# Keeping two more head operands in DRAM between their making and their use

## The chip, the cores and the metric

The kernel runs on one core of a Trainium2 chip. The metric is the device time of one execution in microseconds. Before the change the median of three runs is 1178.21 us (1176.94 to 1178.62). A core has TensorE (PE) for matmuls, VectorE (DVE), ScalarE (ACT), GpSimd (POOL) and SyncE (SP); in this kernel SP issues the loads from DRAM and POOL the stores to it.

## The reference

One layer of a hybrid decoder trunk: 1024 tokens, 1024 channels, float32. The input is normalised and modulated, then one large projection makes the operands of two mixers that run side by side: HGRN2 with 8 heads and GLA (gated linear attention) with 4. Each GLA head has a query, a key (128 channels each), a value (256 channels), an output gate, and a decay alpha for every token and key channel:

```python
log_a = jax.nn.log_sigmoid((ga @ alpha_w + alpha_b)) / GLA_GATE_TAU
# per head: S_t = diag(exp(log_a_t)) S_{t-1} + k_t v_t^T,  o_t = S_t^T (scale * q_t)
o = chunked_gated_linear_attention(q, k, v, log_a, GLA_HEAD_K ** -0.5)
o = rms_norm(o, norm_w)
return o.reshape(B, T, GLA_VAL) * jax.nn.silu(gz)
```

Both mixers' outputs are projected, merged by sigmoid gates, projected once more, added to the input and normalised. Heads are counted from 0 here: the third GLA head is head 2, the fourth head 3.

## The kernel before

**Stages.** Features lie on the partitions, 1024 tokens along a row, so an operand of one head (query, key, decay) is one tile of 128 x 1024 float32, 512 KB. After the normalisation the kernel makes the queries of all heads and the first two keys, and stores them in DRAM (qk_d). Then one stream of jobs runs, `stream.go()`: 14 half products of a first value stage, four jobs for output gates of heads 0 and 1, two jobs for the keys of heads 2 and 3 (`gla_k`), 14 half products of a second value stage, 14 of a third stage, and more gate jobs. Afterwards come the merge stages (L1422) and the output stage (L1599).

Each stage of 14 half products forms one large matrix product from seven smaller ones, numbered 1, 2, 5, 3, 6, 7, 4 in this order (L32), each in two halves (`Vjob`, L1912). A half product is 24 matmuls of 128 x 512 at L2000. A float32 operand is split for PE in two parts: a cast on ACT makes the high part (L211) and a subtraction on DVE the low part (L212). Products 1, 2 and 3 of a half have to split only the weights, two parts; the others also the activations, four parts.

**Side work.** Between the jobs' pieces, `weave` (L881) advances generators: the heads one after another (`gla_attention`, L998, then the HGRN2 heads), sums of weights for the later value stages (`v_sums`, L1819: loads at L1829, sums from L1831, stores at L1839), the decays of heads 2 and 3 (`alpha_side`, L934), and sums for the merge stages (`prepare`, L1280). It counts units, one for each piece of a job, four to a half product. A head begins with copies and products of query and decay (L657 to L661), then 64 small score matmuls (L665) that read the key; it ends with an inverse root of the squares of its outputs (`inverse_root`, L985: split at L202 and L203, matmuls L992 and L993, ACT at L994 and L995). A head, when its values are done with, issues the loads of the next head's operands (`load_qk`, L1050, DMA at L1054).

**The slots.** All large tiles live in 46 slots of 4 KB a partition (`Slots`, L37). `get` takes the slot that has been free for longest, `free` returns one; a tile that is being stored counts as freed four units later in that order, though it can be taken at once. A transfer or an instruction that writes a slot waits for the last reader or store of what lay there.

**Look-ahead.** `Stream.ahead` (L853) loads and splits jobs before their turn. For a job that isn't the running one, a load is issued only if the free slots reach the tiles it loads plus four, a split only if they reach its parts plus one:

```python
if d > loads or d > 0 and room() < job.raws + 4:
    break
...
if d > preps or d > 0 and room() < job.parts + 1:
    break
```

`v_sums` waits for eight free slots, `alpha_side` for six, `prepare` for eleven; `prepare` stands still through the second and most of the third stage.

**Order.** After the first part of the program, instructions are put on their engines' queues by the framework's own scheduling, from program order, priorities (evictions of the value stages are preferred) and what it holds ready, except where the kernel pins them. Each engine then takes its queue in order, SP and POOL too.

**Keys and decays.** Queries of all heads and keys of heads 0 and 1 lie in DRAM until `load_qk`. Key 3 does too (k3_d). Key 2 stays in its slot from the end of its job until head 2 ends; the decays of heads 2 and 3 stay in theirs from `alpha_side` on.

Of the kernel before, what the change touches and what calls it, by code (L numbers as in the profile page):

```python
# [10 lines left out]
F32 = mybir.dt.float32  # L11
# [5 lines left out]
P = 128  # L17
D = 1024
T = 1024
# [70 lines left out]
def hybrid_trunk_kernel(  # L90
# [6 lines left out]
    nc = tc.nc  # L97
# [5 lines left out]
    dp = ctx.enter_context(tc.tile_pool(name="dram", bufs=1, space=bass.MemoryType.DRAM))  # L103
# [3 lines left out]
    S = Slots(sp, N_SLOTS)  # L107
# [7 lines left out]
    def mtile():  # L115
        cnt[0] += 1
        return ps_m.tile([P, 512], F32, tag="m", name=f"pm{cnt[0]}")
# [197 lines left out]
    NG = 6  # L315
# [39 lines left out]
    g_state = {}  # L355
# [31 lines left out]
    def mm_alpha(pz, h, sl):  # L387
        for n in range(2):
            nc.tensor.matmul(pz, aw4[:, n, h * P:h * P + P], ga4[:, sl], start=(n == 0), stop=(n == 1))
# [116 lines left out]
    qk_d = [dp.tile([P, T], F32, name=f"qk{f}") for f in range(NG)]  # L506
# [395 lines left out]
    alphas = {}  # L902
# [6 lines left out]
    def alpha_half(half):  # L909
# [21 lines left out]
            nc.scalar.activation(alphas[h][:, sl], m[:, h, :], AF.Exp, scale=1.0 / TAU)  # L931
        S.free(z, m)

    def alpha_side(pair):  # L934
        zs = {}
        while len(S.free_list) < 6:
            yield 1
        for h in pair:
            zb = zs[h] = S.get([T])
            for th in range(2):  # L940
                pz = mtile()
                mm_alpha(pz, h, slice(th * 512, th * 512 + 512))
                nc.scalar.activation(zb[:, th * 512:(th + 1) * 512], pz, AF.Identity,
                                     bias=vec[:, R_AB + h:R_AB + h + 1])
            yield 2
        S.free(ga4, aw4)
        for h in pair:
            m = alphas[h] = S.get([T])
            nc.vector.tensor_scalar_min(m, zs[h], 0.0)
            nc.vector.scalar_tensor_tensor(zs[h], m, 2.0, zs[h], ALU.mult, ALU.subtract)  # L950
            yield 2
        for h in pair:
            nc.scalar.activation(zs[h], zs[h], AF.Exp)
        yield 3
        for h in pair:
            nc.scalar.activation(zs[h], zs[h], AF.Ln, bias=one_t)
            nc.vector.tensor_sub(alphas[h], alphas[h], zs[h])
            yield 2
        for h in pair:
            nc.scalar.activation(alphas[h], alphas[h], AF.Exp, scale=1.0 / TAU)  # L960
            S.free(zs[h])
        yield 3

    def silu_done(store, key):
# [33 lines left out]
    def gla_attention(h):  # L998
# [29 lines left out]
        if h < 3:  # L1028
            load_qk(h + 1)
# [15 lines left out]
                settle(qk, ("z", h, vh))  # L1045
        S.free(*sq.values())

    k3_d = dp.tile([P, T], F32, name="k3")

    def load_qk(h):  # L1050
        for f, key in ((h, "q"), (4 + h, "k")):
            if f < NG or h == 3:
                t = g_state[key, h] = S.get([T])
                nc.sync.dma_start(t, qk_d[f] if f < NG else k3_d)  # L1054

    def gla_k_done(h):
        def f(ps):
            t = S.get([T])
            for th in range(2):
                nc.vector.tensor_copy(t[:, th * 512:th * 512 + 512], ps[th])  # L1060
            if h == 3:
                nc.gpsimd.dma_start(k3_d, t)
                S.free(t, sent=True)
            else:
                g_state[("k", h)] = t
        return f

    def col(c0, w=P):
# [946 lines left out]
    def first_head():  # L2015
        for h in range(4):
            start_side(gla_attention(h))

    vjobs[0][10].begins = lambda: load_qk(0)
    vjobs[0][12].begins = first_head  # L2020

# [23 lines left out]
    def front():  # L2045
        alpha = [alpha_half(half) for half in range(2)]
        for i, _ in enumerate(first_group()):
            if i < 10 and i % 2 == 0:
                next(alpha[0], None)
            if i == 15:  # L2050
                for _ in make_ga(1):
                    pass
                load_wq(0, 0)
                load_wq(1, 0)
            elif i in (16, 17, 18, 20, 22):
                next(alpha[1], None)
            elif i == 19:
                stream.ahead(0, 0, 0)
        for n, z in enumerate(("12", "22")):
            xq[z] = [hT[1, 2 * n + kk] for kk in range(2)]  # L2060
        stream.more.append([v_sums(1), 1, 1, 56])
        stream.more.append([v_sums(2), 1, 1, 56])
        stream.more.append([gate_side(), 4, 1, 300])
        stream.back.append([alpha_side((2, 3)), 1, 1, 86])
        stream.back.append([prepare(), 1, 1, 98])
# [39 lines left out]
```

## Time and profile before

| | |
|---|---|
| median of 3 runs | 1178.21 us |
| the profiled execution | 1176.48 us |
| its span in the trace | 1174.8 us |
| granted PE clock, mean | 0.998 |
| DMA, mean | 209 GB/s, 245.56 MB |
| DVE subtractions at L212 | 92, 1221 ns each |
| ACT casts at L211 | 92, 1048 ns each |

How to read it: the page gives each engine's busy time and share of the span; the windows give the same for chosen stretches; the waits say which engine stood idle until what; the timeline lists instructions in order, with the idle time of the engine before each in square brackets and what ended it. A row with a count such as x2 is several instructions merged. A landing time is from a DMA's issue to its completion.

### The profile page before, as it was taken

The page shows a single profiled execution, that of the slowest core. Times are in us where ns is not written, and L with a number is a line of the kernel's source. Part 1 is how long each engine was busy: PE and PEld are TensorE (multiplying, and loading weights), DVE is VectorE, ACT ScalarE, POOL GpSimd, SP SyncE. Part 2 cuts the span into 40 slices and gives each one's busy share as a digit, 9 for nine tenths or more (in the row PEclk, how much of TensorE's full clock was granted, in tenths as well). Part 3 has the DMA queues.
Part 4 walks back from the last instruction along what each step waited for, and adds up shares of the span by engine and source line. Part 5 has one row for each costly group of instructions (what it writes and reads, how often), then busy time and mean ns, then how long its engine had stood idle before and what let it go on. Part 6 is the DMA issues. An engine that isn't in the chain of part 4 may idle for free.

```text
span 1174.8 us, 20553 instructions
## 1 busy us (share of the span) xinstructions
PE 1148.9 (98%) x8089; PEld 942.3 (80%) x8089; DVE 842.1 (72%) x1316; ACT 646.8 (55%) x963; POOL 138.3 (12%) x285
## 2 busy tenths in 40 slices
PE   7999999999899999999999999999999999999997
PEld 5777888888778888788788888888888888888886
DVE  4755677676686737897697896595543866988994
ACT  5675454284574758646455445566643644534654
POOL 5121111010111101222211110001110000000000
PEclk9999999999999999999999999999999999999999
DMA  9847459486676446988766955156699846435523
GB/s 320 284 151 245 144 193 310 147 281 218 215 247 210 174 142 215 292 279 271 259 205 197 302 164 162 55 172 202 233 321 296 273 155 220 126 109 174 170 95 136
DMA packets 155986, 245.56 MB, mean 209 GB/s; under 512 B 10139, under 2 KB 107473, under 8 KB 155890
## 3 DMA queue, kind: packets, MB, share of 16 engines
q1 hardware_dynamic: 134866, 174.10, 47.3%
q0 software_dynamic: 20976, 70.15, 15.6%
q8 instruction: 63, 1.03, 0.4%
q14 instruction: 33, 0.27, 0.1%
q10 hardware_dynamic: 48, 0.01, 0.0%
HBM read 170.29 MB, written 73.92 MB: 208 GB/s over the span
## 4 chain that ended last, share of the span: by engine, by line
PE 76%; DVE 8%; ACT 7%; DMA 4%; issue 3%; SPq 1%; DVEq 0%; ACTq 0%
PE pd L2000 16%; PE pd L607 15%; PE pd L1422 14%; PE sc_ps L1422 6%; PE pm L1422 6%; PE pd L1599 3%; DMA b<-in_ada_w_dram 2%; PE pd L396 2%; PE pm L834 2%; DMA b<-in_w_in_dram 2%; PE sc_ps L1599 2%; PE pm L836 2%; PE pm L1599 1%; ACT b L211 1%; PE pm L815 1%
## 5 line engine op out<-in xcount | busy, mean ns | idle before, releaser
L607 PE MATMUL pd<-b,b 128*128 128x512 f32 x1248 | 301.2, 395 | 0.0
L607 PEld LDWEIGHTS pd<-b,b 128*128 128x128 f32 x1248 | 230.0, 188 | 48.2
L2000 PE MATMUL pd<-b,b 128*128 128x512 f32 x1008 | 238.4, 393 | 3.8 <-ACT b L211 2.4
L2000 PEld LDWEIGHTS pd<-b,b 128*128 128x128 f32 x1008 | 187.4, 188 | 45.8 <-ACT b L211 2.8
L1422 PE MATMUL pd<-b,b 128*128 128x512 f32 x720 | 169.5, 390 | 0.0
L1422 PEld LDWEIGHTS pd<-b,b 128*128 128x128 f32 x720 | 134.8, 188 | 28.3
L212 DVE TENSOR_TENSOR b<-b,b 128x1024 fp32r<-128x1024 f32 x92 | 110.7, 1221 | 55.0 <-ACT b L211 53.5
L1365 DVE TENSOR_TENSOR b<-b,b 128x1024 fp32r<-128x1024 f32 x56 | 68.1, 1219 | 56.6 <-ACT b L1364 43.3
L211 ACT CAST b<-b 128x1024 fp32r<-128x1024 f32 x92 | 93.6, 1048 | 18.2 <-DMA v<-b 4.3
L1364 ACT CAST b<-b 128x1024 fp32r<-128x1024 f32 x56 | 58.7, 1051 | 68.1 <-PE pm L1422 17.2
L1422 PE MATMUL sc_ps<-b,b 128*128 128x512 f32 x324 | 77.5, 390 | 0.1
L1342 DVE TENSOR_TENSOR b<-b,b 128x1024 fp32r<-128x1024 f32 x48 | 57.8, 1218 | 26.5 <-ACT b L1341 21.7
L1341 ACT CAST b<-b 128x1024 fp32r<-128x1024 f32 x48 | 49.8, 1050 | 39.7 <-PE pd L1422 15.9
L1422 PE MATMUL pm<-b,b 128*128 128x512 f32 x300 | 71.1, 389 | 0.0
L1422 PEld LDWEIGHTS sc_ps<-b,b 128*128 128x128 f32 x324 | 60.6, 188 | 12.9 <-ACT scT L779 0.5
L1422 PEld LDWEIGHTS pm<-b,b 128*128 128x128 f32 x300 | 56.3, 188 | 11.7
L203 DVE TENSOR_TENSOR b<-b,b 128x1024 fp32r<-128x1024 f32 (+1 forms) x37 | 35.7, 977 | 27.5 <-ACT b L202 27.2
L396 PE MATMUL pd<-b,b 128*128 128x512 f32 x192 | 51.8, 403 | 0.9 <-ACT b L202 0.8
L1274 POOL DMA_DIRECT2D ws<-b x64 | 34.6, 540 | 133.3 <-DVE b L1266 48.9
L834 PE MATMUL pm<-scT,b 128*128 128x128 f32 x256 | 47.5, 277 | 2.3 <-DVE b L821 2.0
L726 DVE TENSOR_TENSOR b<-b,tot 128x512 f32<-128x512 f32 x36 | 24.7, 687 | 32.0 <-PE sc_ps L767 30.4
L396 PEld LDWEIGHTS pd<-b,b 128*128 128x128 f32 x192 | 34.3, 188 | 11.9 <-ACT b L202 1.8
(333 smaller groups left out, 1751.9 us busy)
## 6 DMA issues: line engine op xcount, KB each, us to landing
b<-in_w_in_dram SPq DMA_DIRECT2D x64, 512.0 KB, 6.1
ws<-b POOLq DMA_DIRECT2D x64, 256.0 KB, 5.4
b<-ws SPq DMA_DIRECT2D x32, 512.0 KB, 4.1
b<-in_w_in_dram SPq DMA_DIRECT2D x52, 256.0 KB, 4.4
b<-fx SPq DMA_DIRECT2D x24, 512.0 KB, 4.5
b<-in_x_dram SPq DMA_DIRECT2D x16, 512.0 KB, 6.0
b<-in_ada_w_dram SPq DMA_DIRECT2D x32, 256.0 KB, 6.4
v<-b POOLq DMA_DIRECT2D x32, 256.0 KB, 3.5
```

What stands on the lines that cost most here:

```text
L211: held(nc.scalar.copy(hi, src))
L212: nc.vector.tensor_sub(lo, src, hi.bitcast(F32))
L396: nc.tensor.matmul(accs[f], wg(a, d, f), b[d][:, half * 512:half * 512 + 512], start=(d == 0 and n == 0), stop=(d == KT - 1 and n == 2))
L607: nc.tensor.matmul(ps[th][0:w, :], a[:, k, 0:w], b[:, th * 512:(th + 1) * 512], start=(k == 0 and n == 0), stop=(k == KT - 1 and n == 2))
L834: nc.tensor.matmul(o, vch(ch)[:, vh * P:(vh + 1) * P], scT[:, ch, :], start=True, stop=(ch == 0))
L1341: nc.scalar.copy(hi, src)
L1342: nc.vector.tensor_sub(lo, src, hi.bitcast(F32))
L1364: nc.scalar.copy(hi, t)
L1365: nc.vector.tensor_sub(lo, t, hi.bitcast(F32))
L1422: nc.tensor.matmul(o, a[:, sl], c, start=(p in (1, 5) and kt == 0 and n == 0), stop=(kt == 3 and n == 2), skip_group_check=True)
L1599: nc.tensor.matmul(o, a, b, start=(p in (1, 5) and kt == 0 and n == 0), stop=(kt == 3 and n == 2), skip_group_check=True)
L2000: nc.tensor.matmul(st.bank[i], l_[:, i * P:(i + 1) * P], r_, start=(p in (1, 5) and kk == 0 and a == 0 and n == 0), stop=(kk == 1 and a == ...
```

## The change

Key 2 is stored to DRAM when its job ends, in the way that key 3 was already, and its slot is returned; `load_qk(2)` loads it with the query. The decay of head 3 is stored when `alpha_side` has made it, its slot is returned, and `load_qk(3)` loads it after query and key. The decay of head 2 stays where it was.

```diff
+    alpha3_d = dp.tile([P, T], F32, name="alpha3")
+
     def alpha_side(pair):
...
         for h in pair:
             nc.scalar.activation(alphas[h], alphas[h], AF.Exp, scale=1.0 / TAU)
             S.free(zs[h])
+        if 3 in pair:
+            nc.gpsimd.dma_start(alpha3_d, alphas[3])
+            S.free(alphas.pop(3), sent=True)
         yield 3
...
-    k3_d = dp.tile([P, T], F32, name="k3")
+    k_d = {h: dp.tile([P, T], F32, name=f"k{h}") for h in (2, 3)}
 
     def load_qk(h):
         for f, key in ((h, "q"), (4 + h, "k")):
-            if f < NG or h == 3:
-                t = g_state[key, h] = S.get([T])
-                nc.sync.dma_start(t, qk_d[f] if f < NG else k3_d)
+            t = g_state[key, h] = S.get([T])
+            nc.sync.dma_start(t, qk_d[f] if f < NG else k_d[h])
+        if h == 3:
+            alphas[h] = S.get([T])
+            nc.sync.dma_start(alphas[h], alpha3_d)
 
     def gla_k_done(h):
         def f(ps):
             t = S.get([T])
             for th in range(2):
                 nc.vector.tensor_copy(t[:, th * 512:th * 512 + 512], ps[th])
-            if h == 3:
-                nc.gpsimd.dma_start(k3_d, t)
-                S.free(t, sent=True)
-            else:
-                g_state[("k", h)] = t
+            nc.gpsimd.dma_start(k_d[h], t)
+            S.free(t, sent=True)
         return f
```

## The prediction

> **What bounds the kernel now.** The page comes first.
>
> ```profile
> span 1174.8 us, 20553 instructions
> ...
> PE 1148.9 (98%) x8089; PEld 942.3 (80%) x8089; DVE 842.1 (72%) x1316; ACT 646.8 (55%) x963; POOL 138.3 (12%) x285
> ```
>
> TensorE (PE) is busy in 1148.9 of 1174.8 us. The change adds and removes no matmul, so it can win only from the 25.9 us in which PE idles. Next I read the windows of 25 us and looked for those idle microseconds near the change. Columns: the window, then the busy time of PE, weight loads, DVE, ACT and POOL.
>
> ```profile
> 250.00:275.00 25.00, 25.00 (x336) 20.54 (x335) 24.21 (x45) 18.56 (x28) 2.18 (x5) 1.00 0.91 330
> 275.00:300.00 25.00, 24.55 (x140) 21.20 (x139) 11.13 (x16) 7.96 (x13) 1.54 (x3) 1.00 0.47 166
> 300.00:325.00 25.00, 21.23 (x147) 16.18 (x146) 20.44 (x30) 16.74 (x22) 4.84 (x9) 1.00 0.70 237
> 325.00:350.00 25.00, 25.00 (x278) 20.37 (x277) 22.83 (x43) 18.61 (x33) 2.39 (x5) 1.00 0.81 269
> ```
>
> One window stands out: PE idles 25.00 - 21.23 = 3.77 us from 300 to 325. Cut finer:
>
> ```profile
> 300.00:312.00 12.00, 10.61 (x77) 8.24 (x76) 11.63 (x14) 7.31 (x10) 3.24 (x6) 1.00 0.78 263
> 312.00:325.00 13.00, 10.62 (x72) 7.94 (x71) 8.80 (x17) 9.43 (x12) 1.61 (x3) 1.00 0.62 214
> 285.00:300.00 15.00, 15.00 (x98) 13.48 (x97) 5.43 (x7) 4.72 (x8) 0.53 (x1) 1.00 0.21 72
> 325.00:340.00 15.00, 15.00 (x127) 12.16 (x126) 13.37 (x32) 10.95 (x19) 1.07 (x2) 1.00 0.79 249
> ```
>
> There are two stalls: 12.00 - 10.61 = 1.39 us and 13.00 - 10.62 = 2.38 us. In the first stretch DVE is full (11.63 of 12); in the 15 us before, DVE has 9.57 us and ACT 10.28 us to spare. The waits from 296 to 330 name who ended the stalls, and the timeline shows the chain:
>
> ```profile
> SPq L1054 <- PE pd L2000: 15.9, 1, 15.9
> ...
> PE pd L2000 <- ACT b L211: 2.4, 1, 2.4
> ...
> PE sc_ps L665 <- ACT b L211: 1.4, 1, 1.4
> ```
>
> ```profile
> 299.74 6.78 PE L2000 MATMUL pd<-b,b 128*128 128x512 f32 x29
> ...
> 301.00 1.22 DVE L1833 TENSOR_TENSOR b<-b,b 128x1024 f32<-128x1024 f32 x1
> 301.09 0.32 SPq L1054 DMA_DIRECT2D b<-qk  x1
> ...
> 305.78 2.00 ACT L211 CAST b<-b 128x1024 fp32r<-128x1024 f32 x2
> ...
> 307.12 0.64 DVE L661 TENSOR_TENSOR xb<-xb,b 128x256 f32<-128x256 f32 x1
> ...
> 307.91 0.85 PE L665 MATMUL sc_ps<-xb,b 128*32 128x80 f32 x34 [1.39 <-ACT b L211]
> ...
> 308.22 3.50 DVE L212 TENSOR_TENSOR b<-b,b 128x1024 fp32r<-128x1024 f32 x3
> ```
>
> ```profile
> 313.76 1.05 ACT L202 CAST b<-b 128x1024 fp32r<-128x1024 f32 x1 [2.08 <-DVE b L212]
> ...
> 318.46 1.27 ACT L994 ACTIVATE b<-pm,eps_t 128x512 f32<-128x512 f32 x2
> ...
> 322.47 1.05 ACT L211 CAST b<-b 128x1024 fp32r<-128x1024 f32 x1
> ...
> 323.57 0.51 PE L2000 MATMUL pd<-b,b 128*128 128x512 f32 x1 [2.38 <-ACT b L211]
> ```
>
> Read it thus. The second value stage runs its half products one after another, 24 matmuls each. At 306.5 (299.74 + 6.78) the second half of product 2 ends, and the next job, the first half of product 5, has no split operands: their two ACT casts (L211) run only from 305.78, the DVE remainders (L212) from 308.22. PE's queue meanwhile holds head 2's first score matmuls (L665), which also wait for DVE L661 (307.76). Those late L212s hold back ACT L202, the split inside head 1's inverse root; that root's ACT work (L994, then L995) stands ahead of the cast for product 3 at 322.47, and PE waits the second time.
>
> **Why the splits are late.** I walked the 46 slots of the pool through the program, taking each get and free in order, against the kernel's counter of units (four per half product). At unit 114, midway through product 2's first half, the look-ahead wants to split product 5's first half: it has four parts and is allowed only with five slots free (L865). Four are free. At unit 116 (two got back, one spent on a load, one on a head's tile) it is four again. Only at unit 118, when head 1 ends and returns five slots, are both halves of product 5 split at once. The lateness is one missing slot.
>
> **Part 1, two slots freed earlier.** Key 2 is produced at unit 96 and alpha 3 at unit 101; both are kept now until units 127 and 166. The change returns both slots before unit 114. The walk then finds 4 + 2 = 6 free there, at least five, so the split is taken; it needs net 4 - 2 = 2, leaving room for the load at unit 116 (five free, five needed). At unit 118, with q2 and k2 both fetched, 9 - 2 = 7 are free, and the other half is split as before. No other look-ahead decision between units 96 and 166 changes, and from unit 157 on the counts are those of before. Unit 114 comes after 12 of the 18 matmuls below, at 294.7 us, where ACT and DVE are nearly idle:
>
> ```profile
> 291.94 4.38 PE L2000 MATMUL pd<-b,b 128*128 128x512 f32 x18
> ...
> 297.92 0.60 ACT L1019 ACTIVATE b<-pm 128x512 f32<-128x512 f32 x1 [5.09 <-PE pm L836]
> ```
>
> ACT idles 5.09 us until 297.92; the two casts take 2.00 us of it. The two L212s (3.50 / 3 = 1.17 us each, 2.3 in all) fit in DVE's 9.57 us. By the walk they write tiles whose last readers are jobs already over. Covered by that idleness the move costs nothing; without it, at most 2.0 + 2.3 us.
>
> First stall: product 5 can follow at 306.5 and L665 comes behind it, so 1.39 us go. Bounds 0 (L665 stays ahead in PE's order and still waits for L661) and -1.39; I take -1.4, since the jobs precede the head in program order and stand behind it only because their operands were late. Second stall: with 2.3 us of L212 out of the full stretch the whole chain L202 to L211 moves up 2.3 us, but PE arrives 1.4 earlier, so 2.38 - 2.3 + 1.4 = 1.5 would stay. However, in the walk before, the cast at 322.47 writes the slot that the inverse root's own hi part held, so it had to stand behind the root's matmuls; after the change it gets an older slot, and can go ahead of L994. Then nothing stays. Bounds -0.9 and -2.4; I take -1.8, nearer the second, because the slot excuse is gone but the order on ACT isn't known.
>
> What is late next is DVE: 13.37 of 15 us in 325 to 340.
>
> **Part 2, two stores on POOL, two loads on SP.**
>
> ```profile
> L960 ACT ACTIVATE b<-b x2: 1058/1062/1065, 262.0 to 263.4; 128x1024 f32<-128x1024 f32 x2
> ```
>
> ```profile
> L1060 DVE COPY b<-pd x4: 678/680/683, 267.2 to 275.2; 128x512 f32<-128x512 f32 x4
> ```
>
> ```profile
> L1062 POOL DMA_DIRECT2D k<-b x1: 533/533/533, 276.1 to 276.1; - x1
> L1054 SPq DMA_DIRECT2D b<-k x1: 382/382/382, 368.2 to 368.2; - x1
> ```
>
> ```profile
> k<-b POOLq DMA_DIRECT2D x1, 512.0 KB, 6.6
> b<-k SPq DMA_DIRECT2D x1, 512.0 KB, 5.0
> ```
>
> The stores cost POOL 2 x 0.53 us, waiting for ACT at 264.5 and DVE at 268.5. Behind them on POOL stand only the stores of weight sums and key 3; POOL is busy 2.18 of 25 us there. No cost. But key 2's old slot is now handed to the third weight load of the sums at unit 105, and SP issues in order: that load waits for the store, 268.5 + 0.5 + 6.6 = 275.6, with SP's other loads behind it. Its data is first read by L1833, at 301.00; a load of that line takes at most 11.3 us:
>
> ```profile
> DMA to landing us min/median/max: 2.8/6.2/11.3
> ```
>
> 275.6 + 11.3 = 286.9, so 14 us of cover; zero.
>
> k2's load is issued right behind q2's. Both get weight slots of product 2's first half, as q2 did: q2 again near 301.09, k2 at 301.5, landing 306.5 by the key's 5.0 us, before L665 at 307.91 and unneeded earlier. The loads of that line take:
>
> ```profile
> DMA to landing us min/median/max: 3.2/3.9/7.1
> ```
>
> At 7.1 us it would land at 308.6: between 0 and +0.7 us. I take 0, since L665 moves behind product 5.
>
> Alpha 3's load is the third at head 3's start:
>
> ```profile
> 367.75 0.34 SPq L1054 DMA_DIRECT2D b<-qk  x1
> ...
> 371.64 0.65 DVE L658 TENSOR_TENSOR xb<-b,b 128x256 f32<-128x256 f32 x1 [2.96 <-DMA b<-qk]
> ```
>
> ```profile
> 379.93 1.23 DVE L203 TENSOR_TENSOR b<-b,b 128x1024 fp32r<-128x1024 f32 x1
> ...
> 382.33 0.39 PE L993 MATMUL pm<-b,ones_r 128*128 128x512 f32 x1
> ```
>
> L658 multiplies q by alpha, so it now waits for the third load: issue when k3's is done, 368.2 + 0.4 = 368.6, landing 5.0 later at 373.6, 1.9 us after 371.64. Queued behind L658 on DVE are seven more head operations, then head 2's sums and L203, whose lo part PE's L993 needs. L203 ends at 381.16, L993 starts at 382.33: 1.17 us of cover. So 1.9 - 1.2 = +0.7 at worst, 0 if it lands in q's 3.9 us (371.64 - 367.75). I take +0.3.
>
> [...]
>
> **The sum.** -1.4 - 1.8 + 0.3 = -2.9 us. The profiled execution took 1176.48 us (1.68 around its span), so 1173.6; the median of the three runs, 1178.21, lies 1.73 higher, and there the forecast is 1175.3. A measurement of this kernel tells about 0.2%, 2.4 us, from no change.
>
> **Rivals.**
>
> *The wait moves.* PE comes 3 us earlier to a stretch in which DVE has 1.63 us of 15 free and head 2's chain is DVE's; or L665 stays ahead of product 5. Against it: PE idles nowhere from 325 to 350 now. Gain 0 to 2.3 us, and up to 0.7 lost at head 3: 1175.9 to 1178.9. Chance 0.33.
>
> *It doesn't do what it says.* The two slots are spent by other look-ahead before unit 114, and the split stays at 118. The walk speaks against it (the gets in between are fixed in number). Time 1178.2, chance 0.05.
>
> *Slower, at head 3.* The three loads are in order on SP, and each holds the queue until its slot is free: in the quoted waits q2's load held it 15.9 us. If alpha 3's slot is one still read by the half product after the one that held q3's, its load goes out only when that job ends. Its last 12 matmuls are the first of these:
>
> ```profile
> 373.79 8.46 PE L2000 MATMUL pd<-b,b 128*128 128x512 f32 x36
> ```
>
> 12 x 8.46 / 36 = 2.8 us: issue 376.6, landing 381.6, DVE 10.0 us late, less 1.2 of cover 8.8 lost, with the gain of 3.2 a net +5.6: 1183.8. It decides from a landing at 376.0 (lost 3.2) on. Against it: the walk gives alpha 3 a slot of the same job as k3's. Chance 0.12, with reshuffles of order that I can't place.
> [...]
>
> **How the numbers follow.** Forecast 0.50 (all of it faster by over 0.2%), the wait moves 0.33 and no effect 0.05 (within 0.2%), slower 0.12. Low end: both stalls gone in full, and the 0.45 us of PE from 275 to 300 too, 1178.2 - 4.2 = 1174.0, less half a microsecond for the spread of the runs: 1173.5. High end: 1178.9 and the same half: 1179.4; the slower case, 0.12, is left out. The forecast's own range is 1173.5 to 1175.8.
>
> **What would show it.** Right: L211 and L212 for product 5's first half before 300 us, no PE idle from L211 at about 306 and 321, windows 300 to 325 with PE above 24, q2 still issued near 301. Wrong: these casts still after 305; PE idle reappearing in 325 to 400; a DVE wait at L658 of head 3 over 5 us; or PE idle after 400 differing by over 1 us, which nothing here explains.

## The result and the profile after

The kernel after takes 1175.05 us (1174.07 to 1175.54) beside 1178.53 us of the kernel before: a ratio of 0.9969, 95% interval 0.9958 to 0.998, so 3.5 us less. In a later series it took 1174.53 us, ratio 0.9966 (0.9954 to 0.9979).

The page of the kernel after, its span and engines:

```profile
span 1173.6 us, 20556 instructions
...
PE 1148.3 (98%) x8089; PEld 942.9 (80%) x8089; DVE 842.0 (72%) x1316; ACT 647.3 (55%) x963; POOL 139.4 (12%) x287
```

PE does the same work. Its span is only 1.2 us shorter than that of the profiled execution before, which lay 1.7 us under its own median. Two things keep the spans from showing the 3.5 us. PE reached product 2 1.14 us later in the profile after (293.08, in the timeline below, beside 291.94). It loses this in the first 25 us, where the two programs are the same; the first of these rows is of before, the second of after, and the third number from the end is the granted clock:

```profile
0.00:25.00 25.00, 17.62 (x88) 13.97 (x88) 11.43 (x27) 13.05 (x25) 14.72 (x57) 0.93 0.98 311
...
0.00:25.00 25.00, 16.39 (x83) 13.43 (x84) 10.29 (x26) 13.16 (x25) 14.83 (x57) 0.86 0.96 308
```

And 1.0 us is lost again later: 0.7 us between 711 and 719 us, over half of it in a wait of PE for ACT L792 (0.8 us, 0.4 before), and the rest behind the last matmul; what lengthens them stays open. So I compare the same PE work: from the group of 18 matmuls in product 2's first half to the last such group ahead of head 3, 562 matmul records in each. Before it takes 366.31 - 291.94 = 74.37 us, after 364.15 - 293.08 = 71.07: 3.30 less.

The windows of the kernel after (columns as in the prediction; the first number after the window's length is PE's busy time):

```profile
300.00:325.00 25.00, 23.81 (x165) 18.96 (x164) 21.08 (x32) 17.07 (x23) 5.92 (x11) 1.00 0.82 285
325.00:350.00 25.00, 25.00 (x279) 20.43 (x279) 21.79 (x42) 19.06 (x34) 2.16 (x4) 1.00 0.76 257
```

PE idles 1.19 us from 300 to 325, where it idled 3.77: 2.58 us are won there. (Over the whole stretch PE's idle time falls by 2.71 us, from 3.95 to 1.24. The other 0.6 stands as busy time, 70.42 and 69.83 us; the ends of matmuls are modelled, and part of a wait can lie under them.) The waits and the timeline of that stretch, after:

```profile
PE pm L997 <- ACT b L202: 1.0, 1, 1.0
...
PE pd L2004 <- ACT b L1862: 0.2, 1, 0.2
```

```profile
293.08 4.38 PE L2004 MATMUL pd<-b,b 128*128 128x512 f32 x18
...
293.86 1.99 ACT L211 CAST b<-b 128x1024 fp32r<-128x1024 f32 x2
...
295.80 2.36 DVE L212 TENSOR_TENSOR b<-b,b 128x1024 fp32r<-128x1024 f32 x2
...
306.91 0.66 DVE L658 TENSOR_TENSOR xb<-b,b 128x256 f32<-128x256 f32 x1 [1.28 <-DMA b<-qk]
...
308.87 0.59 ACT L1862 COPY b<-pd 128x512 f32<-128x512 f32 x1 [1.00 <-DMA v<-b]
...
309.36 1.05 ACT L211 CAST b<-b 128x1024 fp32r<-128x1024 f32 x1
...
310.31 1.04 ACT L202 CAST b<-b 128x1024 fp32r<-128x1024 f32 x1
...
311.40 0.73 PE L997 MATMUL pm<-b,ones_r 128*128 128x512 f32 x2 [1.03 <-ACT b L202]
...
316.58 1.06 ACT L1000 ACTIVATE b<-b 128x1024 f32<-128x1024 f32 x1
...
317.54 1.04 ACT L211 CAST b<-b 128x1024 fp32r<-128x1024 f32 x1
...
322.55 1.31 PE L665 MATMUL sc_ps<-xb,b 128*32 128x80 f32 x64
```

The split of product 5's first half stands at 293.86 and 295.80, where ACT and DVE were idle before. Head 2's score matmuls (L665) come behind product 5. Both old stalls are gone. But a new one is there, of 1.03 us: the matmuls of head 1's inverse root (L997, L992 before) wait for the cast L202. The line numbers move by up to seven (L2000 is now L2004, L1054 is L1058).

### The profile page after: what moved, and what is told of

Same layout as the page of the kernel before. It is cut to its first block, busy times and chain, and to the rows that moved or that the text cites. A ratio compares the mean times of both kernels' runs of the same rounds, so it can differ in the third digit from the quotient of the medians.

```text
span 1173.6 us, 20556 instructions
## 1 busy us (share of the span) xinstructions
PE 1148.3 (98%) x8089; PEld 942.9 (80%) x8089; DVE 842.0 (72%) x1316; ACT 647.3 (55%) x963; POOL 139.4 (12%) x287
## 3 DMA queue, kind: packets, MB, share of 16 engines
q8 instruction: 63, 1.03, 0.4%
## 4 chain that ended last, share of the span: by engine, by line
PE 65%; issue 17%; DVE 6%; ACT 5%; DMA 3%; POOL 2%; SPq 1%; POOLq 0%; DVEq 0%; ACTq 0%
PE pd L1426 14%; PE pd L2004 13%; PE pd L607 8%; PE sc_ps L1426 6%; PE pm L1426 6%; PE pd L396 3%; PE pd L1603 3%; PE sc_ps L1603 2%; POOL ws L1278 2%; PE sc_ps L396 2%; PE pm L834 1%; PE pm L1603 1%; PE pm L836 1%; ACT b L211 1%; DVE b L212 1%
## 5 line engine op out<-in xcount | busy, mean ns | idle before, releaser
L607 PEld LDWEIGHTS pd<-b,b 128*128 128x128 f32 x1248 | 230.0, 188 | 48.2
L2004 PE MATMUL pd<-b,b 128*128 128x512 f32 x1008 | 237.9, 393 | 1.7 <-DVE b L364 0.8
L2004 PEld LDWEIGHTS pd<-b,b 128*128 128x128 f32 x1008 | 187.6, 188 | 43.2 <-DVE b L212 1.9
L1426 PEld LDWEIGHTS pd<-b,b 128*128 128x128 f32 x720 | 134.9, 188 | 28.2
L212 DVE TENSOR_TENSOR b<-b,b 128x1024 fp32r<-128x1024 f32 x92 | 110.6, 1220 | 54.9 <-ACT b L211 54.8
L203 DVE TENSOR_TENSOR b<-b,b 128x1024 fp32r<-128x1024 f32 (+1 forms) x37 | 35.7, 975 | 27.4 <-ACT b L202 27.2
L834 PEld LDWEIGHTS pm<-scT,b 128*128 128x128 f32 x256 | 38.5, 191 | 6.7 <-DVE b L821 4.3
```

Of the source, the lines that this page charges most:

```text
L212: nc.vector.tensor_sub(lo, src, hi.bitcast(F32))
L607: nc.tensor.matmul(ps[th][0:w, :], a[:, k, 0:w], b[:, th * 512:(th + 1) * 512], start=(k == 0 and n == 0), stop=(k == KT - 1 and n == 2))
L834: nc.tensor.matmul(o, vch(ch)[:, vh * P:(vh + 1) * P], scT[:, ch, :], start=True, stop=(ch == 0))
L1426: nc.tensor.matmul(o, a[:, sl], c, start=(p in (1, 5) and kt == 0 and n == 0), stop=(kt == 3 and n == 2), skip_group_check=True)
L2004: nc.tensor.matmul(st.bank[i], l_[:, i * P:(i + 1) * P], r_, start=(p in (1, 5) and kk == 0 and a == 0 and n == 0), stop=(kk == 1 and a == ...
```

## The experiments

Each was timed beside the kernel before, whose medians in the three series were 1178.58 to 1178.72 us. In the table, idle is PE's from 300 to 325, and stretch is the same PE work as above. Idle and stretch come from one profile of each kernel; the two profiles of the kernel after differ by 0.24 and 0.26 us, so smaller differences tell nothing.

| kernel | time, us | ratio, 95% interval | idle, us | stretch, us |
|---|---|---|---|---|
| before | | | 3.77 | 74.37 |
| after | 1175.05 | 0.9969 [0.9958, 0.998] | 1.19 | 71.07 |
| key alone | 1177.47 | 0.9993 [0.9985, 1.0002] | 3.49 | 74.84 |
| decay alone | 1177.64 | 0.999 [0.9981, 0.9998] | 3.46 | 74.90 |
| split allowed | 1176.01 | 0.9975 [0.9966, 0.9985] | 2.10 | 72.36 |
| split held | 1175.98 | 0.9975 [0.9965, 0.9984] | 1.78 | 72.13 |
| root tiles swapped | 1176.04 | 0.9976 [0.9967, 0.9985] | 1.80 | 72.05 |
| load held | 1175.56 | 0.9971 [0.9959, 0.9983] | 1.63 | 71.55 |
| split allowed, load held | 1174.36 | 0.9962 [0.9949, 0.9974] | 1.45 | 71.25 |
| key alone, load held | 1175.01 | 0.9968 [0.9956, 0.9981] | 2.09 | 71.56 |
| split allowed, load held, root later | 1174.27 | 0.9963 [0.9951, 0.9976] | 1.64 | 71.40 |
| after, root later | 1174.95 | 0.9968 [0.9956, 0.998] | 1.37 | 71.27 |
| before, load held | 1176.79 | 0.9984 [0.9976, 0.9993] | 2.15 | 73.47 |
| after again | 1174.53 | 0.9966 [0.9954, 0.9979] | 1.43 | 71.33 |

### Is it the one early split?

The theory was that of the prediction: one missing slot delays one split. Four kernels test it. The first has only the key part of the change, the second only the decay part:

> Only key 2 goes to DRAM; decay 3 stays in its slot. One slot comes back instead of two: five are free at unit 114, just enough, so product 5's first half is split there. Theory A (the gain is that one split, done four units earlier, for want of one slot): 2.5 to 3.8 us faster than before, as the whole change, and PE idle from 300 to 325 us below 1.7 us. Theory B (the gain grows with the number of slots, since transfers write older slots and wait less): about half, 1.2 to 2.0 us. Theory C (the order of instructions is drawn anew, and the gain is luck): anything from -3 to +3, unlike the change.

> Only decay 3 goes to DRAM; key 2 stays in its slot. Again five slots are free at unit 114. Theory A: 2.5 to 3.8 us faster than before, as with the key alone. Theory B: about half, 1.2 to 2.0 us. Theory C: anything, and not the same as with the key alone.

The third frees no slot, and relaxes the rule for that one split (job 24 is product 5's first half):

```
spare = 0 if self.prepped == 24 else 1
if d > preps or d > 0 and room() < job.parts + spare:
```

> The kernel before, with nothing kept in DRAM that wasn't; only the look-ahead rule is relaxed by one slot for the split of product 5's first half in the second value stage, so that it is taken at unit 114 with the four slots that are free. Theory A: 2.5 to 3.8 us faster than before, with no store or load added. Theory B: no change, within 0.8 us, or slower, since there are fewer free slots afterwards. Theory C: anything.

The fourth is the kernel after, with that split held to the unit at which it ran before:

```
late = self.prepped == 24 and self.units < 118
if d > preps or late or d > 0 and room() < job.parts + 1:
```

> The kernel after, with both tiles in DRAM and both slots free, but the split of product 5's first half in the second value stage is held back to unit 118, where it was before. Theory A: the gain is gone, within 1.0 us of the time before, and both stalls of PE, at about 306 and 321 us, are back. Theory B: the gain stays, 2.5 us or more faster than before. Theory C: anything.

The theory falls twice. With the key or the decay alone the split is early, yet the stretch gets 0.5 us longer. (Their times are about 1 us shorter all the same, for the one profile of before is of an execution 2.2 us under the median of that series. That is less than the 2.5 us of theory A, and just under the 1.2 of theory B.) With both parts and the split held, 2.2 of the 3.3 us stay, 2.7 us by the times. Theory B falls too: with no slot freed and the split allowed, 2.6 us are won by the times, within what theory A gave. What is missing in the first shows in its timeline, key alone:

```profile
308.15 0.66 DVE L658 TENSOR_TENSOR xb<-b,b 128x256 f32<-128x256 f32 x1 [3.39 <-DMA b<-qk]
...
311.32 1.22 DVE L212 TENSOR_TENSOR b<-b,b 128x1024 fp32r<-128x1024 f32 x1
...
312.57 1.05 ACT L202 CAST b<-b 128x1024 fp32r<-128x1024 f32 x1 [1.02 <-DVE b L212]
...
313.67 1.22 PE L992 MATMUL pm<-b,ones_r 128*128 128x512 f32 x2 [2.52 <-ACT b L202]
...
314.69 2.58 PE L1996 MATMUL pd<-b,b 128*128 128x512 f32 x6
```

The stall ahead of L665 is gone, as forecast, and a stall of 2.52 us stands ahead of the root's matmuls instead: L202 waits for a subtraction of product 5's second half, and that stood on DVE behind L658, which waited 3.39 us for head 2's query. With the decay alone it is ACT that is held first (L657 waits 1.47 us for the query, the casts of product 5 behind it), and PE waits 2.43 us at the same place:

```profile
310.94 1.05 ACT L202 CAST b<-b 128x1024 fp32r<-128x1024 f32 x1 [1.21 <-DVE b L212]
...
312.04 0.89 PE L997 MATMUL pm<-b,ones_r 128*128 128x512 f32 x2 [2.43 <-ACT b L202]
```

The last row of the key alone holds a second loss: six product matmuls take 0.43 us each, where 29 of them took 6.77 us in the kernel after, 0.233 each. The windows of the key alone show why (the column after POOL is the granted clock):

```profile
312.00:314.00 2.00, 0.33 (x1) 0.33 (x2) 2.00 (x4) 1.41 (x2) 0.00 (x0) 0.88 0.96 391
314.00:316.00 2.00, 2.00 (x6) 1.52 (x6) 2.00 (x3) 0.92 (x1) 0.00 (x0) 0.50 0.90 260
316.00:318.00 2.00, 2.00 (x8) 1.62 (x7) 1.93 (x4) 0.46 (x1) 0.54 (x1) 0.77 0.79 199
```

and of the decay alone:

```profile
312.00:314.00 2.00, 1.96 (x5) 1.54 (x6) 2.00 (x3) 1.28 (x1) 0.00 (x0) 0.62 0.82 332
314.00:316.00 2.00, 2.00 (x6) 1.59 (x5) 2.00 (x3) 0.00 (x0) 0.00 (x0) 0.53 0.42 86
```

The clock falls to half at the end of the stall. The loss is 2 x (0.12 + 0.50 + 0.23) = 1.70 us in the one and 2 x (0.38 + 0.47) = 1.70 us in the other, that is 3.4 us at half speed. Without it each stretch would be some 1.2 us shorter than before.

With the split held, the two slots go elsewhere. Head 2's query and key get slots whose last readers ended four units earlier; their loads go out at 289.22 and 289.63, where they went at 301 to 302, and DVE does the head's first products in its idle time:

```profile
295.23 0.65 DVE L658 TENSOR_TENSOR xb<-b,b 128x256 f32<-128x256 f32 x1
...
307.03 1.31 PE L665 MATMUL sc_ps<-xb,b 128*32 128x80 f32 x64
```

L665 doesn't wait at all, and DVE is free for the late splits. So the slots can win by either of two routes.

### The tile that the root's cast writes

With the split allowed and no slot freed, 2.0 us of the stretch were won, less than with the change. Its wait:

```profile
312.81 1.04 ACT L202 CAST b<-b 128x1024 fp32r<-128x1024 f32 x1 [3.26 <-DVE b L212]
...
313.91 0.73 PE L993 MATMUL pm<-b,ones_r 128*128 128x512 f32 x2 [1.09 <-ACT b L202]
```

I walked the slots of all these kernels. The split of product 5's second half reads two raw tiles, the weights first and the activations second, one subtraction each, and frees them. In the kernel after, L202 writes the first of them, and needs the first subtraction only. That ends at 309.42, and L202 starts at 310.31, right behind a cast on ACT; ahead of that cast ACT had stood 1.00 us at L1862, waiting for a store of values (v<-b). In the kernel before, with the key alone and with the split allowed, it gets the second tile and waits for the last subtraction. The look-ahead decides it. With the key alone or the split allowed, the weight load of job 27 takes a slot at unit 118, ahead of the split (in the kernel after it took one at 116); the split is then one slot short, and its own last part goes into the first raw tile. In the kernel before both halves are split at 118, with the same end. (The decay alone leaves L202 the first tile. There the first subtraction itself is late: it runs at 309.69, 17.8 us after the group of 18, where it ran at 308.20, 15.1 us after it, with the change.) The new theory: PE's wait is L202's start against the place of the root's matmuls in PE's order, and the tile sets how early L202 can start. Its rival: the tile is indifferent, and the number of free slots counts. Four kernels:

```
lo, hi = (S.get([T], F32R) for _ in range(2)) if stream.units == 119 else (None, None)
hi, lo = split(sq, hi, lo)
```

> The kernel after, with the two tiles of head 1's inverse root exchanged: its hi part (ACT L202) now gets the tile that its lo part had, which is the last raw tile that the split of product 5's second half read, and the lo part gets the first raw tile. No count of slots, no load and no decision changes. Theory (the root's tile): L202 must now wait for the last L212 of that split, which ends at 311.7 in the kernel after, so it starts about 1.4 us later than 310.3, PE's wait ahead of L997 grows from 1.0 to about 2.4 us, and the time is about 1.4 us over the kernel after: near 1176.4. Rival (which tile it gets is indifferent, only the number of free slots counts): 1175.0, as the kernel after.

The other three hold the load, in the look-ahead's rule, to unit 118 or 120:

```
wait = self.loaded == 27 and self.units < 120
if d > loads or wait or d > 0 and room() < job.raws + 4:
```

> The kernel after, with the weight load of job 27 held from unit 116 to unit 118. Head 2's query then gets a raw tile of the early split (last read at 298.2) and not the weights of a half product that runs to about 302, so its load goes out about 4 us earlier, and its key's stays near 302. Theory (the root's tile): the root's cast keeps the tile it has after, so at least the gain of the kernel after stays: 1174.0 to 1175.1, the lower end if the earlier head operands take the last 1.0 us of waiting ahead of L997. Rival (it is the look-ahead loads that the freed slots let out early): holding this load gives back what they won, about 1 us, near 1176.

> The kernel before with two decisions of the look-ahead set by hand and no slot freed: the split of product 5's first half is allowed at unit 114 (as in the run above that did this alone) and the weight load of job 27 is held to unit 120. With the load held, the root's hi part gets the first raw tile of the split of product 5's second half and not its last. Theory (the root's tile): L202 comes about 1.9 us earlier than 312.8, the 1.1 us of PE's wait ahead of the root's matmuls go, and the time is near the kernel after without any change in DRAM: 1174.9. Rival (the tile is indifferent): 1176.0, as with the split alone.

> The kernel with the key part of the change alone, and with the weight load of job 27 held to unit 120. The split of product 5's first half is early there already; with the load held, the root's hi part gets the first raw tile of the second half's split and not the last. Theory (the root's tile): L202 comes 1 to 1.9 us earlier than 312.6, PE's wait ahead of L992 falls from 2.5 to between 0.6 and 1.5 us, and the time from 1177.5 to 1175.6 to 1176.5. Rival (the tile is indifferent, one freed slot is too few): 1177.5 as with the key part alone.

With the tiles exchanged, L202 starts 1.5 us later, measured from the first group of 18 (18.76 beside 17.23), and now waits for the last subtraction:

```profile
311.41 1.05 ACT L202 CAST b<-b 128x1024 fp32r<-128x1024 f32 x1 [0.34 <-DVE b L212]
```

PE's wait didn't grow where it was expected, because the scheduling put 49 product matmuls ahead of the root's and not 42; it came out further on:

```profile
PE pm L998 <- ACT b L202: 1.0, 1, 1.0
PE pd L2005 <- ACT b L1863: 0.8, 1, 0.8
```

The stretch is 0.7 to 1.0 us longer than in the two profiles of the kernel after, and the time 1.0 to 1.5 us (1176.04 beside 1175.05 and 1174.53, with intervals that overlap); 1.4 were expected. With the split allowed and the load held, both by hand, the whole gain is there without a byte more in DRAM, and L202 starts 2.0 us earlier than with the split alone (17.56 beside 19.55, expected 1.9):

```profile
310.29 1.04 ACT L202 CAST b<-b 128x1024 fp32r<-128x1024 f32 x1 [1.26 <-DVE b L212]
```

But the 1.1 us of PE's wait, which were to go, did not: it is 1.14 us, with 43 product matmuls ahead of the root's where there were 52. What went is most of the waiting behind the root, 1.0 us before and 0.3 now. The key alone gains 2.5 us by the held load, more than the 1.0 to 1.9 expected: PE's wait falls only to 2.09 us, but the clock stays at 1.00. In the kernel after, the held load brought nothing: head 2's query came 4 us earlier, and L202 started where it did. Its time, 1175.56, lies between what the theory (1174.0 to 1175.1) and the rival (near 1176) gave.

One sum comes out the same over these profiles. Take L202's start from the first group of 18, take off 0.233 us for each product matmul ahead of the root's and the recorded wait: 17.23 - 42 x 0.233 - 1.03 = 6.41 in the kernel after. With the split allowed it is 6.34 (19.55, 52, 1.09), with the key alone 6.42 (20.36, 49, 2.52), with the decay alone 6.40, with the tiles exchanged 6.37, with the load held 6.41, with the split allowed and the load held 6.40, with the key and the load held 6.41. This is little more than bookkeeping: up to the root's matmuls PE waits for nothing but L202. It doesn't show what sets L202's start; that the tile can, the exchange of the tiles shows. Each of these kernels also has its own order of instructions from the scheduling (42 to 52 product matmuls ahead of the root's), so theory C is not excluded for the differences of a few tenths among them.

### Is the last wait worth removing?

The root's four matmuls are moved back by some ten product matmuls with a lower priority; in the first of the two kernels ACT, DVE and SP keep their orders:

```
with tc.high_priority(offset=-30 if stream.units == 121 else 0): nc.tensor.matmul(pn, ones_r, hi[:, sl], start=True, stop=False)
with tc.high_priority(offset=-30 if stream.units == 121 else 0): nc.tensor.matmul(pn, ones_r, lo[:, sl], start=False, stop=True)
```

> The run with two look-ahead decisions set by hand (split allowed at 114, load held to 120), and beside that the four norm matmuls of head 1's inverse root moved back in PE's order by some ten product matmuls (0.233 us each), to the end of product 5's first half; ACT, DVE and the loads keep their orders. Theory (PE's wait is the start of ACT L202 against the place of the root's matmuls in PE's order): 10 x 0.233 = 2.3 us more work stands ahead, so the 1.1 us of waiting goes, and the time falls by up to 1.1 from 1174.4: 1173.3. Rival (the chain behind the root sets the end: its log and exponential, then the casts for the next half products): the wait turns up ahead of the product matmuls a few us later and the time stays near 1174.4.

> The kernel after, with the same four matmuls of head 1's inverse root moved back in PE's order by some ten product matmuls. Theory: PE's 1.0 us of waiting ahead of L997 goes and the time falls by up to 1.0 from 1175.05: 1174.0 to 1174.4. Rival (the chain behind the root sets the end): 1175.05, and the wait shows ahead of the product matmuls near 321.

Neither gains. The waits of the first, then of the second:

```profile
PE pm L995 <- DVE b L203: 1.0, 1, 1.0
PE pd L2002 <- DVE b L212: 0.6, 1, 0.6
```

```profile
PE pd L2004 <- ACT b L1862: 1.1, 1, 1.1
PE pm L998 <- DVE b L203: 0.2, 1, 0.2
```

L202's wait is gone, and the same microsecond is waited for the next links: the low part of the root, and the casts and evictions on ACT behind its logarithm and exponential. The chain sets the end here, not the place. Last, the held load alone in the kernel before, and the kernel after once more:

> The kernel before with one decision changed: the weight load of job 27 is held from unit 116 to unit 120. The slot that it leaves lets the split of product 5's first half go at unit 116 (near 302) and not at 118, and the root's hi part gets the first raw tile of the second half's split. No slot is freed. Theory (early split plus the root's tile): both hold here, so the time comes near the run that set both by hand: 1174.4 to 1175.5. Rival (it takes the slots that the change freed, or the split at 114): 1177.5 to 1178.5.

> The kernel after once more, unchanged, so that it stands beside the others on the same chip: 1175.05 within 0.6.

The held load lets the split go at unit 116 and gives the root the first raw tile, and PE does not wait for L202. Still only 1.9 us are won, between what the theory and its rival gave. The waits show a third way to be late:

```profile
ACT xb L657 <- DMA b<-qk: 2.8, 1, 2.8
...
PE pd L2001 <- ACT b L211: 1.4, 1, 1.4
```

Head 2's query now gets a raw tile of the split of product 5's first half, so its load waits for that split and goes out at 307.78; ACT stands 2.8 us at L657, with the root's logarithm and the next casts behind it.

Which kernel is fastest stays open within 0.7 us: after, 1174.53 and 1175.05; split allowed with the load held, 1174.36; their intervals overlap.

## Why the prediction held, and what in it did not

**The total.** Forecast -2.9 us, measured -3.5 (-3.30 over the same PE work). That the total comes so near is in part luck: two of its three terms came out by other ways than given, and the profiles also hold a loss of 0.7 us near 715 that was not forecast. From product 2 to the end they show only 2.3 us; why the medians show 3.5 is open (see the clock, at the end).

**First stall, -1.4.** Right, with its mechanism: the split at 293.86 is taken from idle engines, product 5 follows at once, L665 stands behind it.

**Second stall, -1.8.** The wait at that place fell from 2.38 to 0.16 us, 2.2 less. The chain did move up, by more than the 2.3 us forecast: counted from the group of 18, L202 starts 4.6 us earlier and the cast for product 3 6.1 us. The argument from the slot did not come true: the cast at 317.54 writes an older slot, but still stands behind L1000 (L995 before) on ACT, where the prediction let it go ahead of L994. And the step "What is late next is DVE" in 325 to 340 failed: PE idles nowhere there. What is late next is ACT's L202, at 311.40, with 1.03 us. Net it is -1.2 of recorded idle, and the prediction's rival, that the wait moves, is partly true, in another place. The term is near its size for other reasons than those given.

**The cause, "one missing slot".** This step failed. The walk of the slots was right for the kernel after, and the early split is where its gain begins (allowed alone it wins 2.0 us of the stretch). But one slot gives that split too, and wins nothing measurable with the key and 1.0 us with the decay. The second slot, added to the key's, lets job 27's load go at unit 116, which leaves the root's cast a tile that is read out one subtraction earlier. And head 2's query, for which DVE waits 1.28 us in the kernel after and 3.39 with the key alone, holds up less. How much of the gain each of the two brings was not measured apart. The prediction saw a slot's last reader as the reason for the late cast at 322.47 and didn't ask the same of L202, though the quoted row had its wait of 2.08 us for L212.

**The key's load, 0.** It goes out ahead of the query's, at 302.00 and 302.42, and not behind it, and the query now lands 4.5 us after its issue where it took 3.2. That is the 1.28 us for which DVE waits at L658 (306.91). In the kernel after it costs nothing that shows: with the query 4 us earlier (load held) L202 starts where it did. With the key alone it does cost.

**Head 3, +0.3.** It is 0. The rows of the kernel after:

```profile
366.46 0.42 SPq L1061 DMA_DIRECT2D b<-alpha  x1
...
373.14 0.66 DVE L658 TENSOR_TENSOR xb<-b,b 128x256 f32<-128x256 f32 x1 [6.62 <-DMA b<-alpha]
374.43 1.20 DVE L1035 TENSOR_TENSOR b<-b,b 128x1024 f32<-128x1024 f32 x1
...
378.00 1.23 DVE L203 TENSOR_TENSOR b<-b,b 128x1024 fp32r<-128x1024 f32 x1
...
380.17 0.39 PE L998 MATMUL pm<-b,ones_r 128*128 128x512 f32 x1
```

The load itself is dearer than forecast. L658 starts 7.55 us after the first of the head's loads and not 3.89, so 3.7 us later, where 1.9 was forecast. But head 2's sum (L1035) is now ahead of the head's other products on DVE, L203 ends at 379.23, and L998 at 380.17 doesn't wait: 0.9 us of cover are left. The rival "slower at head 3" doesn't occur. The wait of 6.62 us is over the 5 us that the prediction named as a sign of being wrong, and PE pays nothing for it; another of its signs, PE above 24 us from 300 to 325, is missed too, with 23.81, by the new stall.

**The stores, 0.** Right. Both stand on POOL at 265.90 and 269.89, and the third weight load of the sums did wait for the key's store, 1.9 us. Ahead of it SP had stood 5.2 us for the store of the decay, whose slot the load at L1945 got; the prediction had no such wait.

```profile
269.89 0.54 POOL L1068 DMA_DIRECT2D k<-b  x1 [3.45 <-DVE b L1067]
...
273.15 1.39 SPq L1833 DMA_DIRECT2D b<-in_w_in_dram  x2
```

It goes out at 273.15, and its sums run at 302.14, 9.06 us after the group of 18, as before (301.00 after 291.94). The store of alpha lands 4.9 us after its issue, those of key 2 and key 3 after 3.2 and 7.5, the least and the most here:

```profile
L1068 POOL DMA_DIRECT2D k<-b x2: 531/534/537, 269.9 to 277.3; - x2
...
DMA to landing us min/median/max: 3.2/5.4/7.5
```

For alpha 3's load the prediction took the key's 5.0 us; L658, which waits for it, starts 6.7 us after its issue.

## What to carry to other kernels

A pool that hands out the slot that has been free for longest can turn an early or late `get` into another instruction's wait: after a change of the counts, walk the slots and ask of each cast near a stall whose last reader it now waits for. A freed slot is worth what the look-ahead does with it, and the same gain may be had by one held load and one relaxed rule. And a stall taken from one place is only won when the next link of the chain is early too: give the next late instruction its name and its time before counting it.

## What the runs showed of the hardware

In two of these kernels a stall of PE cost more than its length. After recorded stalls of 2.52 us (key alone) and 2.43 us (decay alone) the granted clock was 0.50 for 3.4 us, by the windows shown above, and 1.70 us were lost each time. After 2.38 us (before) and 2.09 us (key alone, load held) it was 1.00 in every window from 300 to 325. What decides between the two, the length alone or something else, these runs don't show.

The clock may also be part of why the medians differ by more than the profiles. Of the 62 executions of the kernel before in the three series, 32 have a mean clock under 0.996, and their medians lie 1.0 to 1.7 us above those of the others; of the 13 of the kernel after none does. That the stall of 2.38 us halves the clock in those 32 was not shown, since none of them has a profile, and it can't be all: the kernel before with the load held has no such stall in its profile (the longest wait of PE from 300 to 325 is 1.4 us), and yet 6 of its 11 executions lie under 0.996.
